# Spacer tiles between the SBUF pools of a hybrid decoder layer, so that its large buffers begin at multiples of 256 bytes

## Chip, cores and metric

One core of a Trainium2 chip runs the whole layer in one launch. The metric is the device time of one execution in microseconds; the median of the runs counts.

## The reference, cut to what matters

One decoder layer on 256 tokens of width 2048, all in float32. First comes a gated mixer: one input projection (`h @ w_in`) feeds a sparse attention and a stick-breaking attention, both are projected, gated and merged, and `w_o` projects the result. Then cross-attention into 256 memory tokens (`w_cq`, `w_ck`, `w_cv`, `w_co`). Last comes a mixture of 32 experts, of which every token uses two:

```
for gi in range(N_GROUPS):
    a = jnp.einsum("nd,edf->nef", hn, w_eg[gi])
    u = jnp.einsum("nd,edf->nef", hn, w_eu[gi])
    y = y + jnp.einsum("nef,efd->nd", jax.nn.silu(a) * u * combine[:, gi, :, None], w_ed[gi])
```

and a final RMSNorm. The weights of one expert are three matrices of 4 MB each, so all experts together are 384 MB (of 1024 x 1024 KB) that are read from HBM once.

## The kernel before

**Front (projections and attention).** The projections run slab by slab. A weight chunk of 1 MB (128 partitions x 8192 bytes) comes by a DMA into a buffer of the pool `wpool` (six of 8192 bytes a partition). `split` makes of each half of it a high part `wh` on ScalarE (L175) and a low part `wl` on VectorE (L176), float32r tiles of the pool `whl` (three of each, 4096 bytes). `k_steps` (L250 to L252) issues three TensorE matmuls of 512 columns for each 128x128 block: high by high, high by low, low by high. There are 124 such chunks and 24 matmuls on each, 2,976 in all. Attention work is mixed in between by the class `Pump`, and its tiles lie in the pool `att`. Activations lie in `big`, twenty buffers of 4096 bytes a partition (helper `a4`).

**Routing** (L941 to L1025) works on small tiles of the pool `rt` and picks the experts' tokens. TensorE is kept turning with matmuls on a constant (`wp<-ctb`, L958, L995), as it is at the very start with a zeroed tile (`wp<-zt`, L658).

**Experts.** After routing the pools `att` and `whl` are closed and their bytes are given to three new pools: `mo` (small tiles of the expert loop, such as `pg_`, `pT`, `h`), `wleft` (four buffers of 8192 bytes) and `wright` (three, from the upper end of SBUF). Expert weights come in chunks of 1 MB, in the fixed order of `wnext`, into thirteen buffers in turn:

```
slots = [wpool] * 6 + [wleft] * 4 + [wright] * 3 + [None] * EXTRA
```

so of every 13 successive loads six go to `wpool`, four to `wleft` and three to `wright`. Seven chunks are put into pairs of `big` buffers instead (`lent`, tile `wa`). The loads are issued from SyncE's queue (L160), at most eight at a time: the next one is issued when the one eight before it has landed. A buffer is free for its next load when the matmuls that read it (`gu<-w,xt` L1156, `dd<-w,h` L1183) are done. The framework's planner orders each engine's queue, and may put a load whose buffer is free ahead of one whose buffer isn't.

**Where the buffers lie.** Tiles are placed one behind the other, each size rounded up to 32 bytes. The pools on the left follow in the order in which they are opened, those with `side="right"` grow down from the upper end. By the tiles' sizes, in bytes of a partition: the pool `cst` ends at 26208 = 102 x 256 + 96. `big` (20 x 4096) and `wpool` (6 x 8192) begin at 26208 and 108128, 96 past a multiple of 256. `sm` and `rt` take 6208 bytes, so `att` begins at 163488, 160 past one. `mo` begins there too and takes 7808 bytes, so `wleft` begins at 171296, 32 past one. The upper end lies at 229344, 224 past one, and so do all buffers of `whl` and `wright`. The constant `ctb` happens to lie at 18688, a multiple of 256, and `zt` in a buffer of `big`.

Of the kernel before, what the change touches and what calls it, by code (L numbers as in the profile page):

```python
# [12 lines left out]
F32 = mybir.dt.float32  # L13
# [7 lines left out]
P = 128  # L21
# [114 lines left out]
def tile_block(ctx: ExitStack, tc: tile.TileContext, A, out, stop=None, dbg=None):  # L136
# [5 lines left out]
        manual.enter_context(tc.manual_schedule())  # L142

    cst = ctx.enter_context(tc.tile_pool(name="cst", bufs=1))
    big = ctx.enter_context(tc.tile_pool(name="big", bufs=20))
    wpool = ctx.enter_context(tc.tile_pool(name="wpool", bufs=6))
    ps = ctx.enter_context(tc.tile_pool(name="ps", bufs=4, space=bass.MemoryType.PSUM))
    sm = ctx.enter_context(tc.tile_pool(name="sm", bufs=4))
    rt = ctx.enter_context(tc.tile_pool(name="rt", bufs=1))
    att_stack, whl_stack = ExitStack(), ExitStack()  # L150
    att = att_stack.enter_context(tc.tile_pool(name="att", bufs=2))
    whl = whl_stack.enter_context(tc.tile_pool(name="whl", bufs=3, side="right"))
# [516 lines left out]
    for j, _ in enumerate(xT_split(xt[0], 0, 0, XL)):  # L669
        n, jj = divmod(j, 2)  # L670
# [374 lines left out]

    att_stack.close()
    whl_stack.close()
    mo = ctx.enter_context(tc.tile_pool(name="mo", bufs=2))
    wleft = ctx.enter_context(tc.tile_pool(name="wleft", bufs=4))
    wright = ctx.enter_context(tc.tile_pool(name="wright", bufs=3, side="right"))  # L1050
    slots = [wpool] * 6 + [wleft] * 4 + [wright] * 3 + [None] * EXTRA
    loaded, taken = [0], [0]
# [264 lines left out]
```

## Time and profile before

| | |
|---|---|
| median of 3 runs | 1760.94 us (1760.21 to 1763.62) |
| the profiled execution | 1762.8 us |
| its span, first to last instruction | 1761.0 us |
| TensorE busy | 1498.5 us (85%) |
| VectorE / ScalarE busy | 572.7 us (33%) / 453.1 us (26%) |
| moved by DMA | 551.89 MB, mean 313 GB/s |

The busy share of an engine is an average over stages with different limits; the page also cuts the span in 40 slices of 44 us, which is where to read what limits each stage. A busy TensorE includes matmuls that wait for their pipeline. The time of the profiled execution is 1.8 us more than its span.

### The profile page before, as it was taken

What the parts mean: (1) busy time and instruction counts of PE and PEld (TensorE: products, weight loads), DVE (VectorE), ACT (ScalarE), POOL (GpSimd) and SP (SyncE); (2) the same over time, 40 slices, a digit from 0 to 9 for tenths busy, and PEclk for the clock granted to TensorE, in tenths of its full rate; (3) what the DMA queues carried; (4) which work ended last, traced back from release to release, by engine and by line L of the source; (5) the groups of instructions that cost most, each with busy time, mean ns of one, the idle gap of its engine ahead of it and who ended that gap; (6) DMA issues with size and microseconds to landing.
All of it is one profiled execution on the core that took longest, in us unless ns stands there. A gap on an engine that the chain in (4) does not pass through costs nothing. (4 is left out here: it accounts for less than half of the span.)

```text
span 1761.0 us, 18604 instructions
## 1 busy us (share of the span) xinstructions
PE 1498.5 (85%) x7605; PEld 862.1 (49%) x7607; DVE 572.7 (33%) x972; ACT 453.1 (26%) x671; POOL 17.1 (1%) x26
## 2 busy tenths in 40 slices
PE   9999999999999999999776876867867758768665
PEld 6877778888888888885321311312212213213111
DVE  5656544444555556564020110200301202102002
ACT  5535455644344455651000000000000000000002
POOL 0000000000000000000000000000000000000002
PEclk9999999999999999999998998998999899899888
DMA  8653334455555644767999999999999999999996
GB/s 349 255 215 140 120 124 164 151 183 191 186 177 187 236 172 166 298 251 304 420 420 421 420 421 421 420 421 420 421 420 421 420 421 420 421 421 420 421 421 256
DMA packets 83657, 551.89 MB, mean 313 GB/s; under 512 B 9456, under 2 KB 14064, under 8 KB 19056
## 3 DMA queue, kind: packets, MB, share of 16 engines
q1 hardware_dynamic: 82928, 548.55, 78.2%
q0 software_dynamic: 640, 2.11, 0.3%
q8 instruction: 62, 1.02, 0.2%
q14 instruction: 27, 0.22, 0.0%
HBM read 548.52 MB, written 2.10 MB: 313 GB/s over the span
## 5 line engine op out<-in xcount | busy, mean ns | idle before, releaser
L1156 PE MATMUL gu<-w,xt 128*32 128x512 f32 x1992 | 395.5, 690 | 180.1 <-DMA w<-in_w_eu 112.6
L176 DVE TENSOR_TENSOR wl<-w,wh 128x1024 fp32r<-128x1024 f32 (+1 forms) x250 | 303.3, 1216 | 268.4 <-ACT wh L175 268.1
L175 ACT CAST wh<-w 128x1024 fp32r<-128x1024 f32 (+1 forms) x250 | 259.5, 1041 | 308.0 <-PE acc L252 289.3
L1156 PEld LDWEIGHTS gu<-w,xt 128*32 128x32 f32 x1992 | 84.4, 123 | 466.8 <-DMA w<-in_w_eu 202.9
L250 PE MATMUL acc<-wh,xhi 128*128 128x512 f32 x672 | 272.9, 407 | 1.3 <-ACT wh L175 1.3
L251 PE MATMUL acc<-wl,xhi 128*128 128x512 f32 x672 | 266.1, 396 | 0.4 <-DVE wl L176 0.4
L252 PE MATMUL acc<-wh,xlo 128*128 128x512 f32 x672 | 266.4, 396 | 0.0
L1183 PE MATMUL dd<-w,h 128*32 128x512 f32 (+1 forms) x1056 | 186.6, 597 | 23.7 <-DMA w<-in_w_ed 22.0
L1173 DVE TENSOR_TENSOR h<-h,tp 128x256 f32<-128x256 f32 x16 | 6.7, 421 | 557.4 <-ACT h L1172 557.4
L1163 ACT COPY gs<-gu 128x512 f32<-128x512 f32 x16 | 9.4, 585 | 588.5 <-PE gu L1156 588.5
L250 PEld LDWEIGHTS acc<-wh,xhi 128*128 128x128 f32 x672 | 127.0, 189 | 33.1 <-issue 3.1
L252 PEld LDWEIGHTS acc<-wh,xlo 128*128 128x128 f32 x672 | 126.9, 189 | 29.8 <-issue 0.6
L251 PEld LDWEIGHTS acc<-wl,xhi 128*128 128x128 f32 x672 | 127.1, 189 | 28.8 <-DVE wl L176 1.6
L1183 PEld LDWEIGHTS dd<-w,h 128*32 128x32 f32 x1056 | 44.4, 111 | 120.4 <-issue 57.6
L178 ACT ACTIVATE ds<-dd,cw 128x512 fp32r<-128x512 f32 (+1 forms) x33 | 22.2, 674 | 275.2 <-PE dd L1183 216.3
L179 DVE SCALAR_TENSOR_TENSOR ds<-dd,cw,ds 128x512 fp32r<-128x512 f32 (+1 forms) x33 | 24.3, 735 | 166.7 <-ACT ds L178 166.7
L1094 PE MATMUL yp<-ds,pT 128*128 128x512 f32 (+1 forms) x132 | 48.0, 447 | 26.6 <-ACT ds L178 25.1
L250 PE MATMUL acc<-wh,oh 128*128 128x512 f32 x160 | 63.8, 399 | 0.0
L251 PE MATMUL acc<-wl,oh 128*128 128x512 f32 x160 | 63.2, 395 | 0.0
L252 PE MATMUL acc<-wh,ol 128*128 128x512 f32 x160 | 63.2, 396 | 0.0
L1094 PEld LDWEIGHTS yp<-ds,pT 128*128 128x128 f32 x132 | 20.2, 192 | 68.6 <-ACT ds L178 53.0
L250 PE MATMUL acc<-wh,mh 128*128 128x512 f32 x128 | 51.2, 400 | 0.0
(311 smaller groups left out, 1189.2 us busy)
## 6 DMA issues: line engine op xcount, KB each, us to landing
w<-in_w_eg SPq DMA_DIRECT2D x126, 1024.0 KB, 19.8
w<-in_w_ed SPq DMA_DIRECT2D x124, 1024.0 KB, 19.9
w<-in_w_eu SPq DMA_DIRECT2D x123, 1024.0 KB, 19.8
w<-in_w_in SPq DMA_DIRECT2D x75, 1024.0 KB, 4.9
w<-in_w_o SPq DMA_DIRECT2D x16, 1024.0 KB, 4.8
w<-in_w_bra SPq DMA_DIRECT2D x8, 1024.0 KB, 4.9
w<-in_w_brb SPq DMA_DIRECT2D x8, 1024.0 KB, 4.9
wa<-in_w_eu SPq DMA_DIRECT2D x10, 512.0 KB, 11.8
```

Source lines behind the costliest of these rows:

```text
L175: S.copy(hi, src)
L176: V.tensor_tensor(lo, src, hi.bitcast(F32), op=OP.subtract)
L178: S.activation(hi, src, AF.Copy, scale=scale)
L179: V.scalar_tensor_tensor(lo, src, scale, hi.bitcast(F32), op0=OP.mult, op1=OP.subtract)
L250: mm(acc[i], hi[:, j, tok(i)], wh[:, jj], start=q + j == 0, stop=False)
L251: mm(acc[i], hi[:, j, tok(i)], wl[:, jj], start=False, stop=False)
L252: mm(acc[i], lo[:, j, tok(i)], wh[:, jj], start=False, stop=last and j == 3)
L1094: mm(yp, pT[:, i], ds[:, x], start=x == 0, stop=x == 1)
L1156: mm(gu[SL * b:SL * b + SL], XT[g][0][k // 8][:, k % 8, SL * e:SL * e + SL], w[b](j), start=k == 0, stop=k == 15)
L1163: S.copy(gs, gu)
L1173: V.tensor_tensor(h, h, tp[:, :, :, 1], op=OP.mult)
L1183: mm(dd[SL * e:SL * e + SL], H[e // 2][:, f, e % 2], wd[e](f), start=f == 0, stop=f == 3)
```

## The change

Three spacer tiles, which nothing reads or writes, are put in pools of their own: 160 bytes between `cst` and `big`, 192 bytes behind `rt`, and 224 bytes at the upper end ahead of `whl`. And of the two pools that are opened on the left after the attention, `wleft` is now opened before `mo`. By the same arithmetic `big` begins at 26368, `wpool` at 108288, `att` and `wleft` at 163840, and the upper end for `whl` and `wright` is 229120, all multiples of 256; `mo` moves from the lower end of that space to 196608, behind `wleft`. No instruction, load or loop is added, taken away or given another size.

```diff
     cst = ctx.enter_context(tc.tile_pool(name="cst", bufs=1))
+    gap = ctx.enter_context(tc.tile_pool(name="gap", bufs=1))
     big = ctx.enter_context(tc.tile_pool(name="big", bufs=20))
     wpool = ctx.enter_context(tc.tile_pool(name="wpool", bufs=6))
     ps = ctx.enter_context(tc.tile_pool(name="ps", bufs=4, space=bass.MemoryType.PSUM))
     sm = ctx.enter_context(tc.tile_pool(name="sm", bufs=4))
     rt = ctx.enter_context(tc.tile_pool(name="rt", bufs=1))
+    gap2 = ctx.enter_context(tc.tile_pool(name="gap2", bufs=1))
+    gapr = ctx.enter_context(tc.tile_pool(name="gapr", bufs=1, side="right"))
+    for pool, n in ((gap, 40), (gap2, 48), (gapr, 56)):
+        pool.tile([P, n], F32, name="gap")
...
     att_stack.close()
     whl_stack.close()
+    wleft = ctx.enter_context(tc.tile_pool(name="wleft", bufs=4))
     mo = ctx.enter_context(tc.tile_pool(name="mo", bufs=2))
-    wleft = ctx.enter_context(tc.tile_pool(name="wleft", bufs=4))
     wright = ctx.enter_context(tc.tile_pool(name="wright", bufs=3, side="right"))
```

## Rows read from the trace of the kernel before

**Rows 1.** The page's part 2: the span in 40 slices of 44 us.

```profile
PE   9999999999999999999776876867867758768665
...
DMA  8653334455555644767999999999999999999996
GB/s 349 255 215 140 120 124 164 151 183 191 186 177 187 236 172 166 298 251 304 420 420 421 420 421 421 420 421 420 421 420 421 420 421 420 421 421 420 421 421 256
```

**Rows 2.** Busy time by stretch: engines, granted TensorE clock, DMA share, GB/s.

```profile
core 0: us, PE busy (x) PEld busy (x) DVE busy (x) ACT busy (x) POOL busy (x), PEclk, DMA share, GB/s
...
500.00:600.00 100.00, 100.00 (x444) 81.27 (x443) 51.86 (x51) 43.73 (x47) 2.33 (x4) 1.00 0.57 205
...
700.00:800.00 100.00, 99.92 (x478) 82.01 (x477) 61.34 (x92) 54.21 (x91) 0.00 (x0) 1.00 0.73 280
...
1400.00:1600.00 200.00, 145.48 (x790) 46.09 (x791) 19.84 (x43) 9.70 (x17) 0.00 (x0) 0.94 1.01 421
```

**Rows 3.** TensorE's waits, 850 to 1745 us: total us, times, longest us.

```profile
PE gu L1156 <- DMA w<-in_w_eu: 112.6, 84, 1.5
PE gu L1156 <- DMA w<-in_w_eg: 67.4, 53, 1.5
...
PE dd L1183 <- DMA w<-in_w_ed: 22.0, 22, 1.5
```

**Rows 4.** SyncE's queue in order of time, 884 to 966 us: start, us, instruction.

```profile
896.83 0.33 SPq L160 DMA_DIRECT2D w<-in_w_eu  x1
...
914.22 0.33 SPq L160 DMA_DIRECT2D w<-in_w_eg  x1
...
929.19 0.33 SPq L160 DMA_DIRECT2D w<-in_w_eg  x1
...
946.56 0.33 SPq L160 DMA_DIRECT2D w<-in_w_eu  x1
...
961.53 0.33 SPq L160 DMA_DIRECT2D w<-in_w_eu  x1
```

**Rows 5.** The page's part 6, DMA issues: count, KB each, us to landing.

```profile
w<-in_w_eg SPq DMA_DIRECT2D x126, 1024.0 KB, 19.8
w<-in_w_ed SPq DMA_DIRECT2D x124, 1024.0 KB, 19.9
w<-in_w_eu SPq DMA_DIRECT2D x123, 1024.0 KB, 19.8
```

**Rows 6.** SyncE's queue, 801 to 820.2 us.

```profile
801.24 0.33 SPq L160 DMA_DIRECT2D w<-in_w_eg  x1
801.61 0.44 SPq L160 DMA_DIRECT2D w<-in_w_eu  x1
802.10 18.22 SPq L160 DMA_DIRECT2D w<-in_w_eg  x2
```

**Rows 7.** The one DMA issued at 802.10 us, with its time to landing.

```profile
w<-in_w_eg SPq DMA_DIRECT2D x1, 1024.0 KB, 11.1
```

**Rows 8.** SyncE's queue's waits, 740 to 850 us.

```profile
SPq L160 <- PE gu L1156: 20.5, 2, 17.5
```

**Rows 9.** Attention's last matmuls on tiles of `att`: ns min/median/max, first and last start.

```profile
L868 PE MATMUL o<-PT,vm x16: 379/379/483, 767.6 to 776.3; 128*128 128x256 f32 x16
```

**Rows 10.** TensorE in order of time, 600 to 604 us: first and last of 16 matmuls.

```profile
599.80 0.40 PE L252 MATMUL acc<-wh,ol 128*128 128x512 f32 x1
...
603.29 0.39 PE L252 MATMUL acc<-wh,ml 128*128 128x512 f32 x1
```

**Rows 11.** TensorE in order of time, 55 to 62 us: first and last of 32 matmuls.

```profile
58.25 0.28 PE L470 MATMUL gp<-xhi,gs 128*64 128x256 f32 x1
...
61.78 0.28 PE L470 MATMUL gp<-xlo,gs 128*64 128x256 f32 x1
```

**Rows 12.** The matmuls on `zt` and on `ctb` in order of time.

```profile
1.39 4.02 PE L658 MATMUL wp<-zt 128*128 128x512 bf16 x9 [1.39 <-POOL zt L655]
...
807.57 3.62 PE L958 MATMUL wp<-ctb 128*128 128x512 bf16 x8 [0.33 <-issue]
```

**Rows 13.** The same two groups: ns min/median/max of one.

```profile
L658 PE MATMUL wp<-zt x9: 607/631/631, 1.4 to 4.8; 128*128 128x512 bf16 x9
...
L958 PE MATMUL wp<-ctb x8: 634/634/634, 807.6 to 810.6; 128*128 128x512 bf16 x8
```

## Prediction

> **What bounds the kernel now.** I read the slices first, because a change of addresses touches every stage, and the stages have different limits. The reader is to see two regimes with a seam [rows 1]. In slices 0 to 17, up to about 800 us, TensorE is full and the DMA engines are at three to eight tenths. From slice 19 on it is the other way round: DMA is at nine tenths and 420 to 421 GB/s in every slice, and TensorE at six to eight. The table by stretch says the same of the other engines [rows 2]: at 500 to 600 us TensorE is busy for 100.00 of 100 us while VectorE has 51.86 and ScalarE 43.73, and at 700 to 800 us VectorE has 61.34; at 1400 to 1600 us TensorE is busy for 145.48 of 200 us and VectorE and ScalarE for 19.84 and 9.70. Then the waits of TensorE in the second regime [rows 3]: 112.6 + 67.4 + 22.0 = 202.0 us in which it waited for nothing but weights on their way. So the front is as long as TensorE's matmuls, and the expert stage is as long as its weights take to arrive. The seam is read from SyncE's queue below.
>
> **What the change does to each part.** It adds and removes no instruction, so its whole price is what other addresses do to the instructions and transfers that are there, plus what the new order of `wleft` and `mo` does to waits.
>
> *VectorE, ScalarE and GpSimd.* Should the operations on padded tiles become a little shorter or longer, TensorE hides it in the front (at most 61.34 of 100 us busy beside it) and the weight stream hides it among the experts. I cost it at nothing. That cover goes only if one of them grew by more than half.
>
> *TensorE in the front.* Here a changed rate would count in full. Sixteen successive matmuls on `wh` and `wl`, whose buffers lie 224 past a multiple of 256, start 3.49 us apart over 15 intervals, 0.2327 us each [rows 10]. At the granted clock of 1.00 [rows 2], the 2.4 GHz level, 512 columns would take 512 / 2.4 = 0.2133 us. So at most 0.0193 us a matmul, x 2,976 = 57 us, could come from where the columns lie. The nearest row is that of the matmuls with 256 columns from `big`, 96 past a multiple [rows 11]: 3.53 us over 31 intervals, 0.1139 each, so 0.2277 for 512; against that the difference is 0.0050 x 2,976 = 15 us. But these load half as wide a weight block, which may be the whole difference. The one direct comparison is between the matmuls on `zt` (96 past) and on `ctb` (a multiple of 256) [rows 12]: with one matmul's length taken off [rows 13], (4.02 - 0.63) / 8 = 0.424 us and (3.62 - 0.63) / 7 = 0.427 us. Both are 512 / 1.2 GHz, the lower clock level, so at that level an aligned operand gains nothing. I take 0, with 0 and -15 us as the ends; a loss from alignment I exclude, since no row shows an aligned operand slower than its clock.
>
> *The seam.* Moving `wleft` changes which of attention's tiles its first loads must wait for. In what order does this matter? SyncE issues three loads at 801.24, 801.61 and 802.10 us and then nothing until 802.10 + 18.22 - 0.33 = 819.99 us, where the second load of the last row begins [rows 6]. The last of them lands 11.1 us later, at 813.2 [rows 7]. What the queue waits for in between is the first matmul group of the experts, 17.5 us [rows 8]: all thirteen buffers are full, and the next load needs one of them back. So the stream starts when TensorE has used the first weights, and the loads before have 819.99 - 813.2 = 6.8 us in hand. With the new order `wleft` covers attention's tiles one buffer earlier, `PT1` among them, whose last matmul starts at 776.3 us [rows 9], 25 us before the first of the three loads is issued; and `mo` covers tiles of the two mixers that are older still. So I cost the new order at 0. Without that cover each load that missed the seam would add one load to the stream, 2.49 us.
>
> *The weight stream.* This is where alignment can act. By the issues [rows 5] 126 + 124 + 123 = 373 loads of 1 MB go to these buffers; 13 are issued before the seam, which leaves 360. In the stream one load is issued whenever one lands, so the queue's cadence is the rate [rows 4]. From 896.83 to 914.22 there are seven intervals, 17.39 us; from there to 929.19 six, 14.97 us; then seven in 17.37 and six in 14.97 again. That is a cycle of 13, the number of buffers: a fast part of 34.76 / 14 = 2.483 us a load and a slow part of 29.94 / 12 = 2.495. Its order fits the buffers' own, about six of `wpool` (96 past) fast and about seven of `wleft` and `wright` (32 and 224 past) slow. So where a load is written does matter, by 0.012 us or 0.5%, and the mean is 64.70 / 26 = 2.4885 us.
>
> By the Trainium skill ("DMA: Bandwidth & Descriptors", "How a descriptor splits into AXI transactions") a transaction has to start at a multiple of 256 bytes, and a descriptor that does not start there costs the beats from the boundary below it, fetched and not used. By that rule the buffers would pay for 96, 32 and 224 bytes, `wright` most and `wleft` least, and the padding would save about 11 us. The rows do not bear it out: `wpool` is in the fast part and the spread is 0.012 us.
>
> What does a start at a multiple of 256 cost, then? No large buffer has it now. The two ends are all loads fast, 360 x (2.483 - 2.4885) = -2.0 us, and all loads slow, 360 x (2.495 - 2.4885) = +2.3 us. By distance from the boundary 0 is nearest to the slow 32 and 224, by what an aligned start would spare it should be fast; I take the middle, 2.489, so +0.2 us.
>
> **Sum.** 0 (front) + 0 (seam) + 0.2 (stream) = +0.2 us on the profiled execution's 1762.8 us, of which 1761.0 is span and 1.8 lies around it. That execution is 1.9 us above the median of the runs, 1760.94; on the median the sum gives 1761.1, so I forecast 1761.0 us: no change that can be measured. About 0.2%, 3.5 us, is what can be told from none.
>
> **Rivals.**
> 1. *Each row pays for the bytes below its start.* If an 8192-byte row costs time in proportion to its length plus the bytes back to the boundary, the mean over 13 buffers is (6 x 96 + 4 x 32 + 3 x 224) / 13 = 106 bytes, 1.29%, and the padding gives 360 x 2.4885 x 0.0129 / 1.0129 = 11.4 us: 1749.5. For it speaks that the rate depends on the buffer at all. Against it: `wright` would take 192 / 8192 = 2.3%, 0.058 us, more than `wleft`, and the cycle shows one step of 0.012 us and `wpool` on its fast side. A weaker form, in which an aligned start saves one more step below the fast part, gives 2.471 us a load and 360 x 0.0175 = 6.3 us: 1755.
> 2. *TensorE's reads in the front get faster.* The price is the 15 us above: 1746. Against it stands the equal pace on `zt` and `ctb`, for it only that this pair ran at the lower clock.
> 3. *Aligned buffers are slower still (the other side).* The place is the weight stream. 96 past is fast, 32 past and 32 short of a multiple (224) are slow; if rate falls with nearness to the boundary, 0.012 us per 64 bytes, a start on it costs half a step more, 2.501 us: 360 x 0.0125 = 4.5 us, 1765.5. It decides from 2.4885 + 3.5 / 360 = 2.498 us a load.
> 4. *The planner orders the first loads of the experts otherwise*, since a buffer of `wleft` may seem free earlier or later to it. Two loads that miss the seam cost 5 us, 1766; it decides from the second one. Against it: all thirteen buffers are free by 802 and 6.8 us are in hand.
> 5. *The change doesn't do what it says:* the planner or the allocator places the pools otherwise, or the two paces come from the region of SBUF and not from the start within 256. Then nothing moves: 1761.
>
> **How the numbers follow.** The forecast, a stream between the two paces, gets 0.53, and rival 5, which gives the same time, 0.05: the chance of no measurable change is 0.58. Rival 1 gets 0.18 (0.06 in full, 0.12 in the weak form) and rival 2 gets 0.06: faster 0.24. Rival 3 gets 0.12 and rival 4 0.06: slower 0.18. The range goes from 1753, which takes in the weak form of rival 1, to 1766, which takes in rival 3 and the point at which rival 4 decides; left out are the full rival 1, rival 2 and the rest of rival 4, together about 0.16. The likeliest case alone gives 1758.5 to 1763.5.
>
> **What would show it.** Front: 599.80 to 603.29 has its counterpart, and the interval there stays 0.233 us; below 0.229 is rival 2. Seam: the first expert load behind the pause is again issued within 1 us of 820, with 13 loads before it; later, or fewer loads, is rival 4. Stream: the cycle of 13 disappears if the start within 256 made it, and the common interval is between 2.483 and 2.495; 2.46 is rival 1, 2.50 rival 3; if the cycle stays as it is, it is the region and rival 5. I would be wrong above all if a start at a multiple of 256 were a class of its own, outside both paces, since no load of this trace shows one.

## The result, and the profile after

| | before | after |
|---|---|---|
| median | 1761.68 us (4 runs, 1760.21 to 1763.62) | 1734.60 us (4 runs, 1733.41 to 1736.03) |
| span of the profiled execution | 1761.0 us | 1732.8 us |

The ratio is 0.9846, 95% interval 0.9829 to 0.9863: 27 us, 1.5% faster. The forecast was 1761.0 us and no change.

The slices of the changed kernel (page, part 2) have the same two regimes as [rows 1]:

```profile
PE   9999999999999999999776877866867768768665
...
DMA  8664334455555654768999999999999999999997
GB/s 339 267 222 146 122 122 158 158 180 193 192 189 193 233 181 169 307 252 315 423 427 427 426 426 427 427 427 427 427 427 426 427 427 426 427 427 427 427 427 270
```

The one thing that stands out is the last line: 426 to 427 GB/s where [rows 1] have 420 to 421. The same stretches as in [rows 2], with the columns of there, show it too, and that the limits are where they were:

```profile
500.00:600.00 100.00, 100.00 (x454) 82.72 (x453) 54.12 (x54) 44.78 (x48) 2.33 (x4) 1.00 0.59 207
...
1400.00:1600.00 200.00, 152.78 (x846) 51.34 (x840) 25.53 (x51) 11.08 (x19) 0.00 (x0) 0.93 1.01 427
```

In the front TensorE is still busy for 100.00 of 100 us, but it got through 454 matmuls in that stretch instead of 444: it is not less waiting, the matmuls themselves follow one another faster. TensorE's waits in the expert stage (836 to 1718 us) answer to [rows 3]:

```profile
PE gu L1161 <- DMA w<-in_w_eu: 111.7, 85, 1.7
PE gu L1161 <- DMA w<-in_w_eg: 67.1, 53, 1.7
...
PE dd L1188 <- DMA w<-in_w_ed: 17.9, 19, 1.5
```

196.7 us instead of 202.0: the stage still waits for weights. (The lines of the code stand five further down.)

Where do the 28.2 us of span go? The seam divides them. SyncE's queue, 787 to 806.4 us, as in [rows 6]:

```profile
788.47 0.33 SPq L165 DMA_DIRECT2D w<-in_w_eg  x1
788.84 0.43 SPq L165 DMA_DIRECT2D w<-in_w_eu  x1
789.32 17.12 SPq L165 DMA_DIRECT2D w<-in_w_eg  x2
```

The pause ends at 789.32 + 17.12 - 0.33 = 806.11 us instead of 819.99. So **13.9 us come from the front** and the other **14.3 us from the stage behind the pause**, which takes 1732.8 - 806.1 = 926.7 us instead of 1761.0 - 820.0 = 941.0.

Front: TensorE in order of time, 600 to 604 us, first and last of 20 matmuls in a row (compare [rows 10]):

```profile
599.62 0.40 PE L256 MATMUL acc<-wl,mh 128*128 128x512 f32 x1
...
601.93 0.39 PE L257 MATMUL acc<-wh,ml 128*128 128x512 f32 x1
...
603.97 0.39 PE L257 MATMUL acc<-wh,ml 128*128 128x512 f32 x1
```

The last nine intervals take 2.04 us, 0.2267 each, the first ten 0.231. Over the 2,562 intervals under 0.26 us between successive matmuls of this kind behind 60 us, the mean is 0.2278 us, and 0.2325 over 2,563 such intervals before; 0.0047 x 2,976 = 14.0 us, the whole gain of the front.

Stream: SyncE's queue as in [rows 4], two issues 16 loads apart. The changed kernel issues in rounds of four (2.41, 2.45, 2.50 and 2.44 us), so whole rounds are taken:

```profile
869.64 0.33 SPq L165 DMA_DIRECT2D w<-in_w_eg  x1
...
908.88 0.33 SPq L165 DMA_DIRECT2D w<-in_w_eg  x1
```

39.24 us for 16 loads, 2.4525 us each instead of 2.4885; 360 x 0.036 = 13.0 us of the stage's 14.3. Counted through, hold-ups included, it is nearly the same: from the first load of `in_w_ed` (844.55 us before, 830.39 after) to the last one ahead of the gap at the end (1720.07 and 1693.16) 350 intervals take 875.52 us before and 862.77 after, 12.75 less. The other 1.6 us lies in the first loads (0.3) and behind the last of them (1.3). Kernels of one pace differ there by as much: behind that load the kernel before takes 41.0 us, and e9 and e13 below, whose stream has its pace, take 39.9 and 40.1.

### The profile page after: what moved, and what is told of

It is laid out like the page before. It is cut to its first block, busy times and chain, and to the rows that moved or that the text cites. A ratio compares the mean times of both kernels' runs of the same rounds, so it can differ in the third digit from the quotient of the medians.

```text
span 1732.8 us, 18605 instructions
## 1 busy us (share of the span) xinstructions
PE 1474.3 (85%) x7606; PEld 859.2 (50%) x7607; DVE 572.5 (33%) x972; ACT 453.7 (26%) x671; POOL 17.1 (1%) x26
## 5 line engine op out<-in xcount | busy, mean ns | idle before, releaser
L1188 PE MATMUL dd<-w,h 128*32 128x512 f32 (+1 forms) x1056 | 175.3, 584 | 18.7 <-DMA w<-in_w_ed 17.9
```

The source lines that it names most:

```text
L1188: mm(dd[SL * e:SL * e + SL], H[e // 2][:, f, e % 2], wd[e](f), start=f == 0, stop=f == 3)
```

## The experiments

Two questions were open: is it in both places the start at a multiple of 256 that counts, and of which buffers? The theories were put as A (moving columns), B (stationary block), later C (the distance between pools) for the front, and "bytes back to the boundary" against "any start off it" for the stream. All kernels compute the whole layer and differ in spacers and pool order alone. The table has them all; "past" is how far a pool begins past a multiple of 256; the front interval is the mean worked out as above; the rest is the span less the end of the pause. The order `wleft` before `mo` is that of the changed kernel except in e2, e7, e9, e10 and e13.

| kernel | big / wpool / whl past | wleft / wright past | front, us a matmul | pause ends, us | rest, us | time, us |
|---|---|---|---|---|---|---|
| before | 96 / 96 / 224 | 32 / 224 | 0.2325 | 819.99 | 941.0 | 1761.68 |
| after | 0 / 0 / 0 | 0 / 0 | 0.2278 | 806.11 | 926.7 | 1734.60 |
| e1 left only | 0 / 0 / 224 | 0 / 224 | 0.2332 | 821.26 | 926.4 | 1749.51 |
| e2 right only | 96 / 96 / 0 | 32 / 0 | 0.2341 | 824.14 | 934.2 | 1760.09 |
| e3 all 64 | 64 / 64 / 64 | 64 / 64 | 0.2277 | 806.27 | 939.1 | 1746.97 |
| e4 all 32 | 32 / 32 / 32 | 32 / 32 | 0.2278 | 806.10 | 941.9 | 1750.00 |
| e5 all 96 | 96 / 96 / 96 | 96 / 96 | 0.2277 | 805.09 | 940.2 | 1747.05 |
| e6 order only | 96 / 96 / 224 | 160 / 224 | 0.2325 | 818.77 | 939.3 | 1759.82 |
| e7 spacers, old order | 0 / 0 / 0 | 128 / 0 | 0.2278 | 805.13 | 926.8 | 1735.16 |
| e8 all 128 | 128 / 128 / 128 | 128 / 128 | 0.2278 | 805.88 | 938.5 | 1746.11 |
| e9 big as whl | 224 / 96 / 224 | 32 / 224 | 0.2277 | 805.84 | 940.4 | 1747.97 |
| e10 wpool as whl | 96 / 224 / 224 | 32 / 224 | 0.2325 | 819.47 | 942.4 | 1763.78 |
| e13 big 32 short | 192 / 96 / 224 | 32 / 224 | 0.2332 | 822.29 | 940.2 | 1764.35 |

e3, e4 and e7 were timed in four runs each (1746.62 to 1747.41, 1749.80 to 1752.02, 1733.67 to 1736.41; ratios to before 0.9918 [0.9901, 0.9934], 0.9939 [0.9923, 0.9956], 0.9850 [0.9833, 0.9866]), the others once.

**One side at a time (e1, e2).**

```diff
-    for pool, n in ((gap, 40), (gap2, 48), (gapr, 56)):
+    for pool, n in ((gap, 40), (gap2, 48)):      # e1, without the pool gapr
...
+    for pool, n in ((gapr, 56),):                # e2, without gap and gap2, mo before wleft
```

> Only the pools on the left are padded (big, wpool, att, wleft at a multiple of 256); whl and wright stay 224 past. Theory A (each matmul of the front loses time where its moving columns, wh and wl, do not begin at a boundary): the front interval stays at 0.2325 us and the pause before the expert stream ends near 820 us. Theory B (it is the stationary block, xhi and its like in big): the interval falls to 0.2275 us and the pause ends near 806 us. Weight stream, in either: ten of thirteen loads at 2.45 us and the three of wright slower; by the rule of bytes back to the boundary wright takes 2.45 + 8 x 7 beats, about 2.52; if any start off a boundary costs about the same, 2.49.

> Only the upper end is padded (whl and wright at a multiple of 256), the left pools as before. Theory A (moving columns): front interval 0.2275 us, pause ends near 806 us. Theory B (stationary blocks): 0.2325 us, near 820. Weight stream: three of thirteen loads at 2.45 us, ten at 2.48 to 2.50.

Neither A nor B: with the stationary blocks aligned and the columns not (e1) the front takes 0.2332 us a matmul, and the other way round (e2) 0.2341. Each half of the padding alone leaves the front slower than no padding: the pause ends 1.3 and 4.2 us later than before. The stream does gain from the left side alone, and in full: e1's rest is 926.4 us though three of thirteen loads go to 224 past. Its queue shows how:

```profile
889.51 0.33 SPq L164 DMA_DIRECT2D w<-in_w_eg  x1
...
896.99 0.33 SPq L164 DMA_DIRECT2D w<-in_w_eu  x1
...
906.71 0.33 SPq L164 DMA_DIRECT2D w<-in_w_eu  x1
...
916.49 0.33 SPq L164 DMA_DIRECT2D w<-in_w_eu  x1
```

Three loads take 7.48 us, 2.493 each, the next four 9.72, 2.430 each, and then four more 9.78, 2.445. So a load at 224 past is slow, and loads behind it go faster than the mean of the changed kernel, until over all eleven it is 2.453, the same.

**The same distance for all (e3, e4, e5, e8).**

```diff
-    for pool, n in ((gap, 40), (gap2, 48), (gapr, 56)):
+    for pool, n in ((gap, 56), (gap2, 48), (gapr, 40)):   # e3: 64 past
+    for pool, n in ((gap, 48), (gap2, 48), (gapr, 48)):   # e4: 32 past
+    for pool, n in ((gap2, 48), (gapr, 32)):              # e5: 96 past, no gap
+    for pool, n in ((gap, 72), (gap2, 48), (gapr, 24)):   # e8: 128 past
```

> All large buffers 64 bytes past a multiple of 256. If the boundary that counts is 64 bytes, everything is as in the changed kernel: 0.2275 us a matmul, 2.45 us a load, about 1735 us. If it is 256 bytes, the stream is at 2.48 to 2.50 us a load and the front at 0.2325: about 1761 us.

> All large buffers 32 bytes past a multiple of 256. By bytes back to the boundary a load costs 8 rows x 32 bytes more than an aligned one, under 0.01 us: 2.46 us. If any start off a 64 or 256 byte boundary costs the same, 2.494 us, the slow pace of before (its wleft was 32 past), for all thirteen buffers, and the front is at 0.2325 us: about 1762 us.

> All large buffers 96 bytes past a multiple of 256. Theory C (the front loses time where the pools lie at different distances past a multiple of 256 from one another, whatever the distance): the front interval is 0.2275 us, as with all at 0, 32 and 64. A theory by which a boundary counts by itself would give 0.2325. Weight stream: all thirteen buffers at the 2.485 us that wpool had before at the same distance, and no step between the pools; if the step of before came from the region of SBUF, wleft and wright stay slower. About 1747 us.

> All large buffers 128 bytes past a multiple of 256. Front interval 0.2275 us. Stream: by the bytes back to the boundary 4 beats a row, between the 2 beats of 64 and the 7 of 224, so slower than at 64; if any start off the boundary costs one piece more, about the same as at 64 and 96, 2.485 us a load: about 1747 us.

Here the two gains come apart. None of the four has a large buffer at a multiple of 256, and all four have the front of the changed kernel, 0.2277 to 0.2278 us, where the expectations of e3 and e4 had 0.2325 for it; none has its stream. e3, TensorE at 600 to 604 us, first and last of 19:

```profile
599.71 0.39 PE L256 MATMUL acc<-wl,mh 128*128 128x512 f32 x1
...
603.79 0.39 PE L256 MATMUL acc<-wl,mh 128*128 128x512 f32 x1
```

18 intervals in 4.08 us, 0.2267 each, the pace of an aligned kernel at 64 past. In the stream, SyncE's queue of e4 and then of e3, two issues 13 loads apart in each:

```profile
890.43 0.33 SPq L165 DMA_DIRECT2D w<-in_w_eg  x1
...
922.84 0.33 SPq L165 DMA_DIRECT2D w<-in_w_eu  x1
```

```profile
885.56 0.33 SPq L165 DMA_DIRECT2D w<-in_w_eg  x1
...
917.86 0.33 SPq L165 DMA_DIRECT2D w<-in_w_eu  x1
```

32.41 / 13 = 2.493 us at 32 past, 32.30 / 13 = 2.485 at 64. In the same way e5 gives 2.484 (914.40 to 946.69) and e8 2.487 (884.92 to 909.79, ten loads). So the slow pace of [rows 4] is that of 32 and 224, the fast one that of 96, and a start at 0 is a class of its own at 2.453. The bytes back to the boundary don't order them: 128 costs what 64 does, and 32 costs more. And it is the start, not the region of SBUF: e5 has no step between the pools left.

**Only the order, and only the spacers (e6, e7).**

```diff
-    for pool, n in ((gap, 40), (gap2, 48), (gapr, 56)):   # e6: no spacer at all
-        pool.tile([P, n], F32, name="gap")
...
-    wleft = ctx.enter_context(tc.tile_pool(name="wleft", bufs=4))   # e7: spacers kept
     mo = ctx.enter_context(tc.tile_pool(name="mo", bufs=2))
+    wleft = ctx.enter_context(tc.tile_pool(name="wleft", bufs=4))
```

> Only the order of wleft and mo is changed, no spacer. Nothing but wleft moves, from 32 to 160 past a multiple. Front interval 0.2325 us and the pause ending at 820 us as before; stream as before, with wleft at 2.485 instead of 2.493 us at most, which is 1 us in all: 1760 to 1762 us. If the order itself mattered, the pause would end elsewhere.

> The three spacers without the new order: wleft lies behind mo, 128 past a multiple of 256, everything else on a multiple. If a load at a multiple of 256 and one off it only take turns at their own pace (2.45 and 2.49 us), four of thirteen at the slow pace give 2.464 us, 4 to 5 us over the changed kernel. If aligned loads can go at the 2.433 us that they showed beside slow ones and 2.452 us is another limit, the mean of (9 x 2.433 + 4 x 2.486) / 13 = 2.449 us lies under it and the order costs nothing: 2.452 us a load and the changed kernel's time, 1735 us. Front interval 0.2275 us in both.

The new order by itself is worth 1.9 us in a single run (1759.82), of which the 160 past of `wleft` explains the stream's part, about 1 us; I don't read more into it. With the spacers it is worth nothing: e7 takes 1735.16 us with four of thirteen loads at 128 past. Its queue:

```profile
893.59 0.33 SPq L165 DMA_DIRECT2D w<-in_w_eg  x1
...
905.98 0.33 SPq L165 DMA_DIRECT2D w<-in_w_eu  x1
...
913.24 0.33 SPq L165 DMA_DIRECT2D w<-in_w_eg  x1
```

Five loads in 12.39 us, 2.478 each, then three in 7.26, 2.420: 2.456 over the eight. Once more the loads behind the slow ones make up for them. That is what two limits in a row would give: one that depends on where a load is written (some 2.43 us aligned, 2.485 to 2.495 otherwise) and one of 2.453 that does not, with room between them. The expectation of e7 had worked out its time that way. The changed kernel shows the first limit by itself, behind a load that was issued late:

```profile
926.27 0.33 SPq L165 DMA_DIRECT2D w<-in_w_eu  x1
...
938.44 0.33 SPq L165 DMA_DIRECT2D w<-in_w_eg  x1
```

Five loads in 12.17 us, 2.434 each. And by the first limit alone e2, with ten of thirteen loads off the boundary, comes out above the second: (3 x 2.43 + 6 x 2.485 + 4 x 2.494) / 13 = 2.475 us. Its queue, two issues 13 loads apart:

```profile
890.72 0.33 SPq L163 DMA_DIRECT2D w<-in_w_eu  x1
...
922.88 0.33 SPq L163 DMA_DIRECT2D w<-in_w_eg  x1
```

32.16 / 13 = 2.474; the rest is 934.2 us, about half of the gain.

The packets of the kept traces tell what the second limit is. A load is 128 packets of 8192 bytes on 16 DMA engines, 8 on each. From 870 to 1650 us such a packet takes 309.4 ns on average in the changed kernel, e1 and e7, hardly above the shortest of any of these streams, 309. It takes 312.3 in e2, 314.3 in the kernel before and 313.9 to 314.9 in e3, e4, e5 and e8. So 2.453 us is the pace of packets at their shortest (8 x 309 ns = 2.47 us, with the engines' share at 1.01), and starts off the boundary lengthen the packets once most loads have them. They do so in the full stream: in the kernel before 9% of these packets take 310 ns or less there, and 83% in its front (200 to 700 us), where the loads go to the same `wpool`, 96 past. Why they do so stays open.

**Which pools the front compares (e9, e10, e13).** All three start from the kernel before:

```diff
     cst = ctx.enter_context(tc.tile_pool(name="cst", bufs=1))
+    gap = ctx.enter_context(tc.tile_pool(name="gap", bufs=1))     # e9: 32; e13: 24; not in e10
+    gap.tile([P, 32], F32, name="gap")
     big = ctx.enter_context(tc.tile_pool(name="big", bufs=20))
+    gapb = ctx.enter_context(tc.tile_pool(name="gapb", bufs=1))   # e9: 32; e13: 40; e10: 32
+    gapb.tile([P, 32], F32, name="gap")
...
+    gap2 = ctx.enter_context(tc.tile_pool(name="gap2", bufs=1))   # e10 alone, behind rt
+    gap2.tile([P, 32], F32, name="gap")
```

> The kernel before with big put 224 past a multiple of 256, where whl lies, and wpool left at 96 past. The matmul's stationary blocks come from big and its moving columns from whl. Theory C1 (the two reads of TensorE disturb each other when they begin at different distances): front interval 0.2275 us, pause ends near 806 us, 1747 us. Theory C2 (it is what ScalarE and VectorE read in wpool against whl): 0.2325 us, 1761 us. Stream as before in both.

> The kernel before with wpool put 224 past a multiple of 256, where whl lies, and big left at 96 past. Theory C1 (stationary against moving): front interval 0.2325 us, 1761 us and, as wpool's loads are now 224 past, up to 2 us more. Theory C2 (wpool against whl): 0.2275 us and about 1748 us.

> The kernel before with big at 192 past a multiple of 256, 32 bytes short of whl's 224; wpool, att, wleft and wright as before. If only equal distances past a multiple of 256 are free, the front interval is 0.232 us or more (128, 160 and 224 apart gave 0.2325 to 0.234); if the cost grows with the distance between them, it lies between 0.2275 and 0.2325. Stream as before.

e9 at 600 to 604 us, first and last of 19 matmuls, and e10, first and last of 17:

```profile
599.72 0.39 PE L255 MATMUL acc<-wl,mh 128*128 128x512 f32 x1
...
603.82 0.39 PE L255 MATMUL acc<-wl,mh 128*128 128x512 f32 x1
```

```profile
599.79 0.40 PE L255 MATMUL acc<-wl,oh 128*128 128x512 f32 x1
...
603.52 0.39 PE L256 MATMUL acc<-wh,ml 128*128 128x512 f32 x1
```

4.10 / 18 = 0.2278 us against 3.73 / 16 = 0.2331. Moving `big` alone to where `whl` begins, 224 past, gives the whole gain of the front with not one buffer on a boundary: the pause ends at 805.84 us. Moving `wpool` there instead gives nothing in the front; the stream, now at 32 and 224 past throughout, has a rest of 942.4 us, that of e4 (941.9). And with `big` 32 bytes short of the start of `whl` (e13) there is no part of the gain: 0.2332 us, no better than 128, 160 or 224 bytes apart.

## Why the prediction was wrong

**Reading of the two regimes: right.** TensorE's pace sets the front and the weights' arrival the experts, and each of the two gained what its own pace gained: 0.0047 x 2,976 = 14.0 us where the front gained 13.9, and 0.036 x 360 = 13.0 us where the expert stage gained 14.3. VectorE, ScalarE and the seam at nothing: right too; the pause has 13 loads ahead of it in both.

**The failing step in the front** is the sentence "I take 0", which I rested on "the one direct comparison", `zt` against `ctb` [rows 12, 13]. That pair could not show the effect. In both groups block and columns come out of one tile, so they lie at the same distance past a multiple of 256 whatever that distance is, and e3 to e5, e8 and e9 show that this is all the front asks for. The other row told the price within 1.1 us: the matmuls of [rows 11] take block (`gs`) and columns (`xhi`) from `big`, both at 96, and 0.2277 us for 512 columns is what the front now takes. I had it at 15 us, put the difference down to the narrower block, and gave rival 2 a chance of 0.06. Its price was about right and its reason was not: it is not the start on a boundary but the equal distance of `big` and `whl`. The sentence on the other end, "a loss from alignment I exclude", failed too: with one of the two pools put on a boundary the front lost 1.3 us (e1) and 4.2 us (e2). In the changed kernel these matmuls of 256 columns have kept their pace, first and last of 32:

```profile
57.86 0.28 PE L475 MATMUL gp<-xhi,gs 128*64 128x256 f32 x1
...
61.38 0.28 PE L475 MATMUL gp<-xlo,gs 128*64 128x256 f32 x1
```

3.52 us over 31 intervals, 0.1135 against 0.1139.

**The failing step in the stream** is "the two ends are all loads fast ... and all loads slow". I took the two paces that the trace had for the bounds of a third that it did not have, and said in the last paragraph that a class of its own would undo it. It did: 2.453 us lies 0.03 under the fast end. The region of SBUF (rival 5) is excluded by e5, slower aligned buffers (rival 3) by the result, another order of the first loads (rival 4) by the pause.

**Rival 1** came nearest in the stream, 11.4 us where the stage gained 14.3, but its mechanism fell: by the bytes back to the boundary a load at 128 past would cost 0.03 us more than one at 32, and it costs 0.006 less. The rule of the Trainium skill ("DMA: Bandwidth & Descriptors", "How a descriptor splits into AXI transactions") has a start off 256 bytes cost something, and I weighed it too lightly: the rows spoke against its amounts, not against the boundary itself. That section speaks of bytes that are fetched; the starts that were moved here are those to which the loads write, and there the boundary counts. What fits here is a price that hardly depends on the distance, 0.03 to 0.04 us on 128 rows of 8192 bytes.

Rival 1 and rival 2 were priced as if one excluded the other. A gain came in both places. That 1761 - 11.4 - 15 = 1734.6 us is the measured time is luck: the first price was 2.9 us too small, the second 1.1 us too large, and neither gain came by the mechanism it was priced for.

**Open.** That the two reads of TensorE are what disturbs the front is inferred: shown is that it is the distance between `big`, where the blocks are read, and `whl`, where the columns are read. The recorded weight loads of the front keep their length (188.8 ns on average before, 188.2 after, 188.0 in e13); it is the matmuls that come closer together. Why a distance of 256 is free was not tried.

## What to carry to other kernels

When no buffer of a trace has the property that a change brings, the trace bounds nothing on that side: leave the range open there, and ask of each comparison whether it could have shown the effect at all. Give the pools that one matmul reads together the same start within 256 bytes, which costs a spacer of under 256 bytes and was worth 0.8% here. And put most of the buffers that a saturated load stream fills on multiples of 256; up to four of thirteen off it cost nothing.

## What the runs showed of the hardware

- TensorE's float32r matmuls of 512 columns followed each other every 0.2278 us where stationary and moving operands began equally far past a multiple of 256 (0, 32, 64, 96, 128 or 224), and every 0.2325 to 0.2341 us where they did not (32, 128, 160 or 224 from the stationary one's start up to the moving one's, within 256). Padding one of the two made it worse.
- A load of 128 rows of 8192 bytes took 2.453 us in a full stream into starts at a multiple of 256, 2.484 to 2.487 at 64, 96 and 128 past, and 2.493 to 2.495 at 32 and 224 past.
- A few slow loads among aligned ones were made up for: behind them loads took 2.42 to 2.43 us each.
- The rows of such loads, packets of 8192 bytes, took 309 ns in the full stream with all or most starts at a multiple of 256, and 313.9 to 314.9 ns on average with none there; in the half-empty front of the kernel before 83% took 310 ns or less although none of `wpool` began there.
